# Routing tail on whole fp32 operands, with the gate multiply taken off GpSimd, and a sample GLA state that streams through TensorE

## The chip, the cores and the metric

The kernel runs on one core of one Trainium2 chip. The metric is device time in microseconds (us) of one execution; lower is better. The engines of the core are named as in the profile: PE (TensorE), DVE (VectorE), ACT (ScalarE), POOL (GpSimd) and SP (SyncE, which here only issues DMAs).

## The reference, cut to what matters

One inference step of two layers over 512 prompt tokens and 64 sample tokens (8 sequences of 8). Each layer mixes tokens with three branches (windowed attention, gated linear attention called GLA, causal pooling), merges them, normalises, and applies a PEER layer: each token picks 16 of 16384 one-neuron experts for each of 8 heads.

```
q   = x @ w_query                        # 16 tables of 1024x128: 8 heads x 2 halves
s   = q . sub_keys                       # 128 scores per token, head and half
sv, si = top_k(s, 16);  cand = sv[0][:, None] + sv[1][None, :]
cscore, ci = top_k(cand, 16);  g = softmax(cscore);  eidx = cidx[ci]
h = gelu(u_tab[eidx] . x);  y = sum(g * h * v_tab[eidx])

# GLA, per head and chunk; for a sample sequence S starts from state_gla
o = (q*exp(b)) @ S + causal((q*exp(b)) @ (k*exp(-b)).T) @ v
S = exp(b_last) * S + (k*exp(b_last - b)).T @ v
```

All inputs and outputs are fp32.

## The kernel before

A layer goes through two groups of tokens, one after the other. Group G0 holds 256 prompt tokens and the 64 sample tokens (W = 320 columns), group G1 the other 256 prompt tokens. `_p1` runs the mixing branches and the first norm on one group, `_query` the 16 query tables (`pq`) and the top-16 of each. Matmul operands come in two forms. *Split*: `stream` loads a table `raw` of 128x1024, ACT casts it to `whi` (fp32r), DVE or POOL subtracts to make `wlo`, and `mm_into` runs three passes of 8 matmuls (hi·hi, hi·lo, lo·hi). *Whole*: fp32 operands and one pass of 8 matmuls, each of which the trace shows as two records. `G.nat` says which form a group uses; G1 is whole for attention and GLA, split afterwards. The query tables are split, and POOL makes their `wlo` in G1.

PEER is not gathered for most tokens. For the first 384 tokens a dense loop computes all 128 experts of the first key table (`expert_h`: split `ut` table times `x1A`, 24 matmuls of 384 columns, then Gelu on ACT), multiplies each by a dense gate matrix and accumulates `y`; 24 `y` matmuls of 512 columns follow per expert. The remaining 192 tokens go by gathered rows (`Gather`: `choose`, `fetch`, `weigh`), as background work of DVE and POOL.

The dense gate matrix is written by `_spread`, for 128 tokens at a time: 32 steps of 4 tokens. A step makes two one-hot tiles, `jo` (row index) and `io` (column index times gate), multiplies them on PE (L947) and lets ACT copy the result into four tiles `gst0` to `gst3` (L949). After 8 steps ACT issues four DMAs `gd<-gst` (L955). Tokens 0 to 255 are spread in the background while G1 runs (`pool_mul` off: four `tensor_scalar` on DVE, L943, make `io`). Tokens 256 to 383 are spread in the **tail**, the stretch between G1's query and the dense loop (`pool_mul` on: DVE compares, L939, POOL multiplies by the gate, L940). The program order of the tail is: query of G1, `_slots` (select of tokens 256 to 383, and transposes into `selT`), `h` of the first 12 experts (LA), `_spread`, `choose` for the last 128 tokens at a priority that the code sets, dense loop. The scheduler orders each engine's instructions by program order and priority.

The sample part of GLA works per head on `S0`, the states of 8 sequences (128x8x256), loaded by SP, updated in place by DVE (L550) and stored by ACT (L552). `S0` has one buffer, so a head's load waits until the store of the head before has been read out. Each half `dv` of the output reads `S0` with 8 matmuls of 8 columns:

```
mms += [(po[:, HB + b8 * 8:HB + b8 * 8 + 8], S0[:, b8, dc], qd[:, HB + b8 * 8:HB + b8 * 8 + 8])
        for b8 in range(NB)]
```

`S0[:, b8, dc]` (128x128) is the stationary operand and 8 columns of `qd` move. Both layers run the same code, layer 1 about 2410 us later than layer 0.

Of the kernel before, what the change touches and what calls it, by code (L numbers as in the profile page):

```python
# [10 lines left out]
F32 = mybir.dt.float32  # L11
F32R = mybir.dt.float32r
# [94 lines left out]
class Net:  # L107
# [294 lines left out]
def _phase_gla(n, l, oT):  # L402
    tc, nc, c, G = n.tc, n.nc, n.c, n.G
    W, smp = G.W, G.smp
    with tc.tile_pool(name="gla", side="right", bufs=1) as p, tc.tile_pool(name="gla_u", side="right", bufs=9) as up:
# [10 lines left out]
        for i in range(2):  # L416
            a = p.tile([128, 2, 128], F32, name=f"attT{i}")
            s = p.tile([64, 64], F32, name=f"attS{i}")
            nc.gpsimd.memset(a, 0.0)
            nc.gpsimd.memset(s, 0.0)  # L420
            attT.append((a, s))

# [42 lines left out]
        for h in range(4):  # L465
# [33 lines left out]
            if smp:  # L499
# [3 lines left out]
                                        c["rowm"][0:64, :, None].to_broadcast([64, NB, 128]), op=OP.mult)  # L503
            aT, aS = attT[h % 2]
            pa = n.sm("pa")
# [255 lines left out]
def _p1(n, l, G, xs, xres, dsts, opened=None):  # L761
# [3 lines left out]
    with tc.tile_pool(name="mg", bufs=1) as mp, ExitStack() as xc:  # L765
# [161 lines left out]

def _spread(n, gp, t, sT, new_ps, gt0=None):
    nc, c = n.nc, n.c
    io4 = c["iota"][:, None, :].to_broadcast([128, 4, 128])  # L930
    for g in range(128 // GT):
        st = [gp.tile([128, 32, GT], F32, name=f"gst{i}") for i in range(4)]
        for t4 in range(0, GT, 4):
            tt = g * GT + t4
            jo = gp.tile([128, 4, 128], F32, name="jo", bufs=n.job)
            io = gp.tile([128, 4, 128], F32, name="io", bufs=n.job)
            nc.vector.tensor_tensor(jo, io4, sT[:, 1, tt:tt + 4, None].to_broadcast([128, 4, 128]), op=OP.is_equal)  # L937
            if n.pool_mul:
                nc.vector.tensor_tensor(io, io4, sT[:, 0, tt:tt + 4, None].to_broadcast([128, 4, 128]), op=OP.is_equal)  # L939
                nc.gpsimd.tensor_tensor(io, io, sT[:, 2, tt:tt + 4, None].to_broadcast([128, 4, 128]), op=OP.mult)  # L940
            else:
                for k in range(4):
                    nc.vector.tensor_scalar(io[:, k, :], c["iota"], sT[:, 0, tt + k:tt + k + 1],  # L943
                                            sT[:, 2, tt + k:tt + k + 1], op0=OP.is_equal, op1=OP.mult)
            ps = new_ps().rearrange("p (a b) -> p a b", a=4)
            for k in range(4):
                nc.tensor.matmul(ps[:, k, :], jo[:, k, :], io[:, k, :], start=True, stop=True)  # L947
            for i in range(4):
                nc.scalar.copy(st[i][:, :, t4:t4 + 4], ps[:, :, i * 32:(i + 1) * 32].rearrange("p t i -> p i t"))  # L949
            if t4 + 4 < GT:  # L950
                yield
        if gt0 is not None:
            nc.scalar.copy(gt0[:, t * (128 // GT) + g], st[0][:, 0:4, :])
        for i in range(4):
            nc.scalar.dma_start(n.gd[t * (128 // GT) + g, :, i * 32:(i + 1) * 32, :], st[i])  # L955
        yield
# [72 lines left out]
def tile_hybrid_step(ctx, tc, I, O, L):  # L1029
# [59 lines left out]
    for l in range(L):  # L1089
# [14 lines left out]
        sv, siu = _sel_tiles(sa, 3)  # L1104
        n.job, n.pool_mul = 2, False
        _query(n, l, sa, [n.ks(xa[0]), n.ks(xa[1])], G0.tok, G0.W, sv, siu, n.new_mm)
# [24 lines left out]
        _p1(n, l, G1, [n.ks(x32)], xres, lambda t, c0: [(xb[0], xb[1], c0)],  # L1131
            open_xb)
# [22 lines left out]
        def expert_h(i, eng):
            uh, ul = n.stream(I["ut"][l, i], eng)
            ps = n.hring("ps_h")
            for a, (wt, xi) in enumerate(((uh, 0), (uh, 1), (ul, 0))):
                for k in range(8):
                    nc.tensor.matmul(ps[:, 0:TD], wt[:, k * 128:(k + 1) * 128], x1k[xi][k],  # L1160
                                     start=(a == 0 and k == 0), stop=(a == 2 and k == 7))
# [26 lines left out]
        with tc.tile_pool(name=f"dense{l}", bufs=1) as dp:  # L1188
            gt, late = None, []
            for i in range(NE):  # L1190
# [219 lines left out]
```

## Time and profile before

| | |
|---|---|
| median of 3 runs | 4836.3 us (4829.33 to 4840.92) |
| profiled execution | 4858.47 us, of which its span 4856.7 us |
| mean granted TensorE clock | 0.957 |
| PE busy | 4582.4 us (94%) |
| DVE busy | 3853.8 us (79%) |
| ACT busy | 1869.3 us (38%) |
| POOL busy | 1583.2 us (33%) |

Stages of layer 0 in the trace: G0 up to 600 us, its GLA heads from about 251 to 367; query of G0 to 675; G1 to 1208 with the background spread; tail from 1208 to the first `y` matmul at 1406.80; dense loop to about 2400. In layer 1 the GLA heads stand at about 2660 to 2777, the tail from 3628 to 3830. In the windows view a row gives, for a stretch, the busy time of each engine with its count of instructions, then the granted clock of PE as a share of 2.4 GHz (0.50 is 1.2 GHz), the busy share of the DMA engines and GB/s. In a timeline an x16 row is sixteen like instructions run together, and the bracket behind it is idle time ahead of it with what ended it.

### The profile page before, as it was taken

How to read it: one execution, taken by the hardware profiler on the slowest of the kernel's cores; microseconds unless marked ns; L12 is line 12 of the kernel's file. 1: busy time of each engine (PE TensorE's matmuls, PEld its weight loads, DVE VectorE, ACT ScalarE, POOL GpSimd, SP SyncE). 2: the span in 40 equal slices, each digit the busy share in tenths (PEclk: the TensorE clock that was granted, in tenths of full speed). 3: DMA queues.
4: the chain of work that ended last, by engine and by line, in shares of the span. 5: the costliest groups of instructions: out<-in, count | busy, mean ns of one | idle time of the engine just before them, and what ended most of it. 6: DMA issues, size and time to landing. Idle time of an engine off the chain costs nothing. (4 is left out here: it accounts for less than half of the span.)

```text
span 4856.7 us, 71125 instructions
## 1 busy us (share of the span) xinstructions
PE 4582.4 (94%) x26132; PEld 4105.7 (85%) x26132; DVE 3853.8 (79%) x7303; ACT 1869.3 (38%) x3874; POOL 1583.2 (33%) x996
## 2 busy tenths in 40 slices
PE   7999999998889999999999999999988899999998
PEld 6879886798878999999879799777888789999997
DVE  5445698697989999999864456986979899999998
ACT  3424323354433433333343243234544334333333
POOL 0011001111655555555200110011116555555552
PEclk9979999999999999999999799998999999999999
DMA  4324535576469998988723345255664698988986
GB/s 144 108 94 142 175 108 201 169 251 225 154 227 330 327 330 324 334 322 325 268 87 115 96 140 180 88 209 180 234 231 143 245 327 325 334 321 331 327 325 231
DMA packets 363753, 1095.80 MB, mean 226 GB/s; under 512 B 28622, under 2 KB 168398, under 8 KB 313932
## 3 DMA queue, kind: packets, MB, share of 16 engines
q1 hardware_dynamic: 276336, 610.98, 37.9%
q0 software_dynamic: 55296, 402.68, 22.1%
q10 hardware_dynamic: 31772, 77.60, 4.2%
q8 instruction: 206, 3.38, 0.3%
q14 instruction: 143, 1.17, 0.1%
HBM read 1014.01 MB, written 77.52 MB: 225 GB/s over the span
## 5 line engine op out<-in xcount | busy, mean ns | idle before, releaser
L127 POOL TENSOR_TENSOR wlo<-raw,whi 128x1024 fp32r<-128x1024 f32 x288 | 850.1, 2953 | 796.5 <-ACT whi L130 750.7
L130 ACT CAST whi<-raw 128x1024 fp32r<-128x1024 f32 x638 | 666.4, 1048 | 727.8 <-PE ps_mm L182 363.1
L1160 PE MATMUL ps_h<-x1A,whi 128*128 128x384 f32 x4096 | 776.2, 342 | 35.4 <-ACT h L1163 32.5
L1160 PEld LDWEIGHTS ps_h<-x1A,whi 128*128 128x128 f32 x4096 | 729.1, 192 | 56.1 <-ACT h L1163 36.0
L127 DVE TENSOR_TENSOR wlo<-raw,whi 128x1024 fp32r<-128x1024 f32 x350 | 432.2, 1240 | 293.2 <-PE ps_mm L182 144.5
L990 POOL DMA_INDIRECT uvr<-uv,gidx x384 | 437.9, 1140 | 456.2 <-DVE zB L1008 237.9
L1008 DVE SCALAR_TENSOR_TENSOR zB<-uvr,hc,zB 128x1024 f32<-128x1024 f32 x380 | 566.2, 1490 | 4.7
L1001 DVE SCALAR_TENSOR_TENSOR uvr<-uvr,x1B 128x1024 f32<-128x1024 f32 x384 | 490.5, 1277 | 74.7 <-DMA uvr<-uv,gidx 74.5
L1216 PE MATMUL y<-vh,wh 128*128 128x512 f32 x1536 | 476.5, 392 | 5.4 <-ACT vh L130 5.4
L1216 PE MATMUL y<-vl,wh 128*128 128x512 f32 x1536 | 476.9, 392 | 3.8 <-DVE vl L127 3.8
L1216 PE MATMUL y<-vh,wl 128*128 128x512 f32 x1536 | 474.8, 390 | 0.0
L182 PE MATMUL ps_mm<-xa,whi 128*128 128x320 f32 x2400 | 427.4, 329 | 13.4 <-ACT xa L130 13.4
L1205 DVE TENSOR_TENSOR h<-h,gt 128x384 f32<-128x384 f32 x256 | 402.8, 1579 | 28.9 <-DMA gt<-gd 15.2
L182 PEld LDWEIGHTS ps_mm<-xa,whi 128*128 128x128 f32 x2400 | 382.7, 199 | 38.4 <-issue 19.3
L1160 PE MATMUL ps_h<-x1A,wlo 128*128 128x384 f32 x2048 | 400.4, 338 | 0.0
L1160 PEld LDWEIGHTS ps_h<-x1A,wlo 128*128 128x128 f32 x2048 | 361.2, 189 | 0.1
L1216 PEld LDWEIGHTS y<-vl,wh 128*128 128x128 f32 x1536 | 287.7, 188 | 69.7 <-DVE vl L127 6.6
L1216 PEld LDWEIGHTS y<-vh,wl 128*128 128x128 f32 x1536 | 288.5, 188 | 62.6
L130 ACT CAST wh<-h 128x384 fp32r<-128x384 f32 x256 | 130.6, 512 | 547.1 <-PE y L1216 527.2
L1216 PEld LDWEIGHTS y<-vh,wh 128*128 128x128 f32 x1536 | 286.0, 188 | 49.8 <-ACT vh L130 6.0
L1003 ACT ACTIVATE hc<-hc 128x1 f32<-128x1 f32 x384 | 77.5, 203 | 639.8 <-DVE uvr L1001 625.6
L127 DVE TENSOR_TENSOR vl<-vr,vh 128x1024 fp32r<-128x1024 f32 x256 | 316.0, 1235 | 0.0
(339 smaller groups left out, 7686.2 us busy)
## 6 DMA issues: line engine op xcount, KB each, us to landing
raw<-wall SPq DMA_DIRECT2D x468, 512.0 KB, 3.6
raw<-ut SPq DMA_DIRECT2D x256, 512.0 KB, 5.1
vr<-vt SPq DMA_DIRECT2D x256, 512.0 KB, 6.6
gd<-gst ACTq DMA_DIRECT2D x96, 512.0 KB, 5.0
gt<-gd SPq DMA_DIRECT2D x62, 768.0 KB, 12.2
S<-state_gla SPq DMA_DIRECT2D x8, 1024.0 KB, 7.1
s_gla<-S ACTq DMA_DIRECT2D x8, 1024.0 KB, 4.5
uvr<-uv,gidx POOLq DMA_INDIRECT x384, 8.4
```

What stands on the lines that cost most here:

```text
L127: return eng.tensor_tensor(lo, src, hi.bitcast(F32), op=OP.subtract)
L130: return self.nc.scalar.copy(hi, src), self.sub_lo(lo, src, hi, eng)
L182: self.nc.tensor.matmul(ps[:, 0:W], w[wi][:, k * 128:(k + 1) * 128], xs[xi][k], start=(a == 0 and k == 0), stop=(a == len(pa) - 1 and k == ...
L990: self.n.nc.gpsimd.indirect_dma_start(out=r, out_offset=None, in_=self.n.I["uv"], in_offset=bass.IndirectOffsetOnAxis(ap=self.idx[t][:, s: ...
L1001: nc.vector.scalar_tensor_tensor(r[:, 0:1024], r[:, 0:1024], 1.0, self.x[t], op0=OP.mult, op1=OP.mult, accum_out=hc[:, 0:1])
L1003: nc.scalar.activation(hc[:, 1:2], hc[:, 0:1], AF.Gelu)
L1008: nc.vector.scalar_tensor_tensor(acc, r[:, 1024:2048], hc[:, 1:2], acc, op0=OP.mult, op1=OP.add)
L1160: nc.tensor.matmul(ps[:, 0:TD], wt[:, k * 128:(k + 1) * 128], x1k[xi][k], start=(a == 0 and k == 0), stop=(a == 2 and k == 7))
L1205: nc.vector.tensor_tensor(h3, h3, gt[:, :, i % 4, :], op=OP.mult)
L1216: nc.tensor.matmul(y[t][d], wt[:, ts], vt[:, d * 512:(d + 1) * 512], start=(j == 0 and a == 0), stop=(j == NE - 1 and a == 2))
```

## The change

**Whole query in the tail.** `G.nat` is set back to whole at the end of `_p1`, so G1's query uses the raw tables and `xb` becomes one fp32 pair of tiles; its `wlo`, its ACT cast and the DVE subtraction for `xb` go. The sample-side part of `x1A` is then split by ACT and DVE from `xb` (four DMAs before).

**Whole first 12 experts.** A new pair of tiles `x1W` holds the 384 tokens in fp32 (two POOL additions and two ACT copies). The first 12 experts use it with the raw table and 8 matmuls; the other 116 stay split.

**Spread.** One tile `oh` (two buffers) replaces `jo` and `io` (three buffers in the tail, two in the background); one tile `gst` (one buffer) replaces four; one ACT copy of 128x512 per step replaces four of 128x128. In the tail (`act_mul` = 2) two of the four one-hots are scaled by the gate on ACT, two are made by DVE's `tensor_scalar`; POOL takes no part. The tail's spread is issued at priority 250.

**Sample GLA state.** Per head DVE copies the sample queries into a zeroed, padded tile `qm`; 8 matmuls with 64 padded queries stationary move all of `S0` (256 columns each) into one PSUM tile; ACT copies that to `os`; each half then takes one matmul of `os` with a 64-column identity. `S0` is read by those 8 matmuls alone.

```diff
-            return self.stream(self.I["wall"][l, WPOS[name]], self.nc.gpsimd if self.G.fin and name[0] == "pq" else self.nc.vector,
-                               pool, whole=self.G.nat and name[0] != "pq")
+            return self.stream(self.I["wall"][l, WPOS[name]], self.nc.vector,
+                               pool, whole=self.G.nat)
...
+            if smp:
+                nc.vector.tensor_copy(qm.rearrange("p (b j) -> p b j", b=NB)[:, :, 0:8],
+                                      qd[:, HB:W].rearrange("p (b j) -> p b j", b=NB))
+                pso = n.sm("ps_os", (128, 256))
+                for b8 in range(NB):
+                    nc.tensor.matmul(pso[0:NS], qm[:, b8 * NS:(b8 + 1) * NS], S0[:, b8, :], start=(b8 == 0), stop=(b8 == NB - 1))
+                os = p.tile([NS, 256], F32, name="os", bufs=2)
+                nc.scalar.copy(os, pso[0:NS])
...
-                    mms += [(po[:, HB + b8 * 8:HB + b8 * 8 + 8], S0[:, b8, dc], qd[:, HB + b8 * 8:HB + b8 * 8 + 8])
-                            for b8 in range(NB)]
+                    mms.append((po[:, HB:W], os[:, dc], c["ident"][0:NS, 0:NS]))
...
+    G.nat = G.fin
...
-        st = [gp.tile([128, 32, GT], F32, name=f"gst{i}") for i in range(4)]
+        st = gp.tile([128, 128, GT], F32, name="gst", bufs=n.gst)
...
+            oh = gp.tile([128, 2, 4, 128], F32, name="oh", bufs=n.job)
+            w = n.act_mul
+            for k in range(4):
+                gate = sT[:, 2, tt + k:tt + k + 1]
+                if k < w:
+                    nc.scalar.activation(oh[:, 0, k, :], oh[:, 0, k, :], AF.Copy, scale=gate)
+                else:
+                    nc.vector.tensor_scalar(oh[:, 0, k, :], c["iota"], sT[:, 0, tt + k:tt + k + 1], gate,
+                                            op0=OP.is_equal, op1=OP.mult)
...
-            for i in range(4):
-                nc.scalar.copy(st[i][:, :, t4:t4 + 4], ps[:, :, i * 32:(i + 1) * 32].rearrange("p t i -> p i t"))
+            nc.scalar.copy(st[:, :, t4:t4 + 4], ps.rearrange("p t i -> p i t"))
...
+        x1W = [sp.tile([128, 4, TD], F32, name=f"x1W{q}") for q in range(2)]
+        for q in range(2):
+            nc.gpsimd.tensor_tensor(x1W[q][:, :, 0:HB], x1A[0][q][:, :, 0:HB].bitcast(F32), x1A[1][q][:, :, 0:HB].bitcast(F32),
+                                    op=OP.add)
+            nc.scalar.copy(x1W[q][:, :, HB:TD], xb[q][:, :, 0:TD - HB])
...
-        n.job, n.pool_mul = 3, True
+        n.job, n.gst, n.act_mul = 2, 1, 2
...
-        hs = [expert_h(i, nc.gpsimd) for i in range(LA)]
+        hs = [expert_h(i, x1w) for i in range(LA)]
...
+            with tc.high_priority(SPREAD):
+                for _ in _spread(n, gp, 2, sT2, new_y, gt0):
+                    pass
```

The order in which the engines get their instructions moves in three places. The first is PE in layer 0, first head of the sample GLA; `ps_o` is the output of one half, `S_2192` (in the change `S_2196`) the state S0. Before:

```order
L541 MATMUL ps_o<-qd,S 128x64 x2
L541 MATMUL ps_o<-qd,S_2192 128x8 x8
L548 MATMUL ps_S<-vb,klm 128x256 x2
L541 MATMUL ps_o<-attT_1751,vb 128x128 x2
L541 MATMUL ps_o<-attS_1752,vb 128x64
L541 MATMUL ps_o<-qd,S 128x64 x3
L541 MATMUL ps_o<-qd,S_2192 128x8 x8
```

With the change:

```order
L553 MATMUL ps_o<-qd,S 128x64
L538 MATMUL ps_os<-S_2196,qm_1755 64x256 x8
L553 MATMUL ps_o<-qd,S 128x64
L560 MATMUL ps_S<-vb,klm 128x256
L553 MATMUL ps_o<-ct,os 128x64
L560 MATMUL ps_S<-vb,klm 128x256 x2
L553 MATMUL ps_o<-attT_1751,vb 128x128 x2
```

The state is read once, ahead of the end of the first half, where it was read in both halves.

The second is DVE in the tail of layer 0, where `choose` and the spread meet (`rprod`, `rsum`, `gidx` and the MAX rows are of `choose`). Before, from the end of `choose`:

```order
L848 TENSOR_TENSOR rprod<-rstep,si 128x2048
L852 TENSOR_TENSOR rsum<-rprod 128x1024
L852 TENSOR_TENSOR rprod<-rsum 128x512
L852 TENSOR_TENSOR rsum<-rprod 128x256
L854 TENSOR_TENSOR key_13212<-rsum 128x16x8
L981 TENSOR_TENSOR gidx_11382<-key_13212 128x128
L937 TENSOR_TENSOR jo<-ct,selT_12219 128x512
L939 TENSOR_TENSOR io<-ct,selT_12219 128x512
```

With the change, from the top-16 of `choose`'s sixth head:

```order
L815 MAX cv<-s_12359 128x8
L951 TENSOR_TENSOR oh<-ct,selT_11615 128x512
L953 TENSOR_TENSOR oh<-ct,selT_11615 128x256
L960 TENSOR_SCALAR oh<-ct,selT_11615 128x128 x2
L951 TENSOR_TENSOR oh<-ct,selT_11615 128x512
L953 TENSOR_TENSOR oh<-ct,selT_11615 128x256
L960 TENSOR_SCALAR oh<-ct,selT_11615 128x128 x2
L816 MAX_INDEX ciu<-cv,s_12359 128x8
L813 MAX_INDEX ciu<-cv,cand 128x8
```

Before, 29 of the 32 steps stood behind the whole of `choose`; now 11 stand among its top-16 rows and others among its sums.

The third is ACT in the same tail, at the end of the first eight steps (`gst` the collecting tile, `gd` its DMA, `ps_yr` the PSUM result). Before:

```order
L949 COPY gst_12727<-ps_yr 128x32x4
L949 COPY gst_12728<-ps_yr 128x32x4
L949 COPY gst_12729<-ps_yr 128x32x4
L949 COPY gst_12730<-ps_yr 128x32x4
L953 COPY gt_12220<-gst_12727 128x128
L955 DMA gd<-gst_12727 128x1024
L955 DMA gd<-gst_12728 128x1024
L955 DMA gd<-gst_12729 128x1024
L955 DMA gd<-gst_12730 128x1024
L949 COPY gst_12848<-ps_yr 128x32x4
```

With the change:

```order
L958 ACTIVATE oh<-oh,selT_11615 128x128 x2
L965 COPY gst<-ps_yr 128x128x4
L969 COPY gt_11616<-gst 128x128
L971 DMA gd<-gst 128x1024 x4
L958 ACTIVATE oh<-oh,selT_11615 128x128 x4
L1182 ACTIVATE h<-ps_h 128x384
L919 ACT_TABLE_LOAD
L919 ACTIVATE g_12417<-g_12417 128x128
L965 COPY gst<-ps_yr 128x128x4 x3
```

Four tiles released one by one have become a single tile that all four DMAs read, and two scales stand ahead of each copy; four stand between the DMAs and the next copy.

## Rows read from the trace of the kernel before

**Rows 1.** Part 1 of the page: busy time, share of the span, instructions.

```profile
PE 4582.4 (94%) x26132; PEld 4105.7 (85%) x26132; DVE 3853.8 (79%) x7303; ACT 1869.3 (38%) x3874; POOL 1583.2 (33%) x996
```

**Rows 2.** Windows view: G0's GLA, layers 0 and 1, and G1's GLA (900:960).

```profile
300.00:310.00 10.00, 10.00 (x27) 6.86 (x28) 2.72 (x7) 1.09 (x5) 0.00 (x0) 0.50 0.00 0
...
240.00:380.00 140.00, 135.91 (x637) 111.19 (x636) 63.46 (x107) 33.30 (x64) 15.35 (x17) 0.74 0.31 100
2640.00:2780.00 140.00, 135.98 (x644) 111.10 (x643) 60.61 (x101) 28.40 (x56) 14.82 (x17) 0.74 0.30 97
900.00:960.00 60.00, 52.64 (x303) 43.59 (x301) 42.45 (x93) 29.38 (x83) 11.26 (x12) 0.91 0.46 152
```

**Rows 3.** Timeline of PE in the GLA stage: start, us, operation, count.

```profile
262.59 4.86 PE L541 MATMUL ps_o<-qd,S 128*128 128x64 f32 x22
...
324.22 1.84 PE L541 MATMUL ps_o<-qd,S 128*128 128x8 f32 x16
...
367.36 4.36 PE L182 MATMUL ps_mm<-xa,whi 128*128 128x320 f32 x16
```

**Rows 4.** Part 6 of the page: DMA issues, KB each, us from issue to landing.

```profile
gd<-gst ACTq DMA_DIRECT2D x96, 512.0 KB, 5.0
...
S<-state_gla SPq DMA_DIRECT2D x8, 1024.0 KB, 7.1
s_gla<-S ACTq DMA_DIRECT2D x8, 1024.0 KB, 4.5
```

**Rows 5.** Tile view of S in layer 0's G0: duration ns min/median/max.

```profile
L550 DVE SCALAR_TENSOR_TENSOR S<-S,dec,ps_S x32: 472/479/482, 264.5 to 367.9; 128x256 f32<-128x256 f32 x32
```

**Rows 6.** Timeline of PE: a whole table in G1, then the tail of layer 0.

```profile
820.89 12.76 PE L182 MATMUL ps_mm<-oa,raw 128*128 128x256 f32 x58 [0.15 <-DMA raw<-wall]
...
1217.34 2.17 PE L182 MATMUL ps_yr<-xb,whi 128*128 128x256 f32 x16
...
1220.30 0.61 PE L812 MATMUL ps_sc<-key,qT 128*128 128x128 f32 x4
1220.66 1.56 PE L182 MATMUL ps_yr<-xb,whi 128*128 128x256 f32 x11
...
1263.46 1.39 PE L812 MATMUL ps_sc<-key,qT 128*128 128x128 f32 x8
...
1270.57 2.94 PE L1160 MATMUL ps_h<-x1A,whi 128*128 128x384 f32 x16
...
1274.73 2.94 PE L1160 MATMUL ps_h<-x1A,whi 128*128 128x384 f32 x16
...
1340.50 1.12 PE L947 MATMUL ps_yr<-io,jo 128*128 128x128 f32 x8
1341.38 0.42 PE L1160 MATMUL ps_h<-x1A,whi 128*128 128x384 f32 x1
...
1406.80 1.66 PE L1216 MATMUL y<-vh,wh 128*128 128x512 f32 x6 [2.71 <-ACT vh L130]
```

**Rows 7.** Windows view of layer 0's tail: select, choose, spread.

```profile
1270.00:1300.00 30.00, 23.04 (x122) 22.40 (x121) 29.89 (x134) 11.68 (x16) 12.52 (x5) 0.89 0.25 88
1300.00:1333.00 33.00, 30.55 (x177) 30.23 (x175) 32.38 (x66) 14.86 (x25) 23.77 (x11) 0.95 0.38 124
1333.00:1392.00 59.00, 42.24 (x272) 35.87 (x272) 58.73 (x59) 22.45 (x116) 38.12 (x30) 0.94 0.31 118
```

**Rows 8.** Groups of DVE in 1333:1392: count, busy us, mean ns, idle before.

```profile
L939 DVE TENSOR_TENSOR io<-ct,selT 128x512 f32<-128x512 f32 x29 | 43.3, 1494 | 0.0
L937 DVE TENSOR_TENSOR jo<-ct,selT 128x512 f32<-128x512 f32 x29 | 19.7, 679 | 0.0
```

**Rows 9.** Groups of DVE: one sum in 1270:1333, then in 640:860.

```profile
L852 DVE TENSOR_TENSOR rprod<-rsum 128x512 bf16<-128x512 bf16 x6 | 9.1, 1515 | 0.1
...
L852 DVE TENSOR_TENSOR rprod<-rsum 128x512 bf16<-128x512 bf16 x6 | 3.0, 508 | 0.0
```

**Rows 10.** Timeline of DVE in the background spread.

```profile
1090.16 1.10 DVE L943 TENSOR_SCALAR io<-ct,selT 128x128 f32<-128x128 f32 x4
```

**Rows 11.** Groups of ACT in 1333:1392, with idle time by what ended it.

```profile
L949 ACT COPY gst<-ps_yr 128x128 f32<-128x128 f32 x113 | 22.1, 285 | 35.7 <-PE ps_yr L947 23.2 <-DMA gd<-gst 12.3
```

More of the change, by code (lines that the diff above doesn't have):

```diff
@@ L46 @@
 LAGB = -50
+SPREAD = 250
 C_QA, C_KA, C_VA, C_QB, C_KB, C_VB, C_LR, C_GB, C_UC, C_GT = (
@@ L420, in _phase_gla @@
             nc.gpsimd.memset(s, 0.0)
-            attT.append((a, s))
+            qm = p.tile([128, NB * (NS + 8)], F32, name=f"qm{i}") if smp else None
+            if smp:
+                nc.gpsimd.memset(qm, 0.0)
+            attT.append((a, s, qm))
         ps = n.pmm.tile([128, 512], F32, tag="mm", name="ps_lr", bufs=3)
@@ L503, in _phase_gla @@
                                         c["rowm"][0:64, :, None].to_broadcast([64, NB, 128]), op=OP.mult)
-            aT, aS = attT[h % 2]
+            aT, aS, qm = attT[h % 2]
             pa = n.sm("pa")
@@ L929, in _spread @@
     nc, c = n.nc, n.c
-    io4 = c["iota"][:, None, :].to_broadcast([128, 4, 128])
+    iota = lambda w: c["iota"][:, None, None, :].to_broadcast([128, w, 4, 128])
     for g in range(128 // GT):
-        st = [gp.tile([128, 32, GT], F32, name=f"gst{i}") for i in range(4)]
+        st = gp.tile([128, 128, GT], F32, name="gst", bufs=n.gst)
         for t4 in range(0, GT, 4):
             tt = g * GT + t4
[L935 to L944, printed above, removed]
+            oh = gp.tile([128, 2, 4, 128], F32, name="oh", bufs=n.job)
+            w = n.act_mul
+            nc.vector.tensor_tensor(oh[:, 1], iota(1)[:, 0], sT[:, 1, tt:tt + 4, None].to_broadcast([128, 4, 128]), op=OP.is_equal)
+            if w:
+                nc.vector.tensor_tensor(oh[:, 0, 0:w], iota(1)[:, 0, 0:w], sT[:, 0, tt:tt + w, None].to_broadcast([128, w, 128]),
+                                        op=OP.is_equal)
+            for k in range(4):
[5 more added lines that the diff above has]
+                                            op0=OP.is_equal, op1=OP.mult)
@@ L945, in _spread @@
             ps = new_ps().rearrange("p (a b) -> p a b", a=4)
             for k in range(4):
-                nc.tensor.matmul(ps[:, k, :], jo[:, k, :], io[:, k, :], start=True, stop=True)
-            for i in range(4):
-                nc.scalar.copy(st[i][:, :, t4:t4 + 4], ps[:, :, i * 32:(i + 1) * 32].rearrange("p t i -> p i t"))
+                nc.tensor.matmul(ps[:, k, :], oh[:, 1, k, :], oh[:, 0, k, :], start=True, stop=True)
+            nc.scalar.copy(st[:, :, t4:t4 + 4], ps.rearrange("p t i -> p i t"))
@@ L952, in _spread @@
         if gt0 is not None:
-            nc.scalar.copy(gt0[:, t * (128 // GT) + g], st[0][:, 0:4, :])
+            nc.scalar.copy(gt0[:, t * (128 // GT) + g], st[:, 0:4, :])
         for i in range(4):
-            nc.scalar.dma_start(n.gd[t * (128 // GT) + g, :, i * 32:(i + 1) * 32, :], st[i])
+            nc.scalar.dma_start(n.gd[t * (128 // GT) + g, :, i * 32:(i + 1) * 32, :], st[:, i * 32:(i + 1) * 32, :])
         yield
@@ L1104, in tile_hybrid_step @@
         sv, siu = _sel_tiles(sa, 3)
-        n.job, n.pool_mul = 2, False
+        n.job, n.gst, n.act_mul = 2, 1, 0
         _query(n, l, sa, [n.ks(xa[0]), n.ks(xa[1])], G0.tok, G0.W, sv, siu, n.new_mm)
@@ L1125, in open_xb @@
             xbp = xbc.enter_context(tc.tile_pool(name=f"xb{l}", side="right", bufs=1))
-            xb.extend([xbp.tile([128, 4, G1.W], F32R, name=f"xb{i}{q}") for q in range(2)] for i in range(2))
+            xb.extend(xbp.tile([128, 4, G1.W], F32, name=f"xb{q}") for q in range(2))
         n.early = EARLY
@@ L1143, in tile_hybrid_step, with expert_h @@
                 nc.sync.dma_start(x1A[i][q][:, :, 0:HB].bitcast(F32), x1h[i, q])
-                nc.sync.dma_start(x1A[i][q][:, :, HB:TD].bitcast(F32), xb[i][q][:, :, 0:128].bitcast(F32))
+        for q in range(2):
+            n.split(x1A[0][q][:, :, HB:TD], x1A[1][q][:, :, HB:TD], xb[q][:, :, 0:TD - HB])
         x1k = [n.ks(x1A[0]), n.ks(x1A[1])]
         sc, sp = scope(f"sel{l}")
+        x1W = [sp.tile([128, 4, TD], F32, name=f"x1W{q}") for q in range(2)]
+        for q in range(2):
+            nc.gpsimd.tensor_tensor(x1W[q][:, :, 0:HB], x1A[0][q][:, :, 0:HB].bitcast(F32), x1A[1][q][:, :, 0:HB].bitcast(F32),
+                                    op=OP.add)
+            nc.scalar.copy(x1W[q][:, :, HB:TD], xb[q][:, :, 0:TD - HB])
+        x1w = [n.ks(x1W)]
         sv, siu = _sel_tiles(sp, 2)
-        n.job, n.pool_mul = 3, True
+        n.job, n.gst, n.act_mul = 2, 1, 2
         yc, n.py = scope(f"ps_y{l}", space=PSUM)
         new_y = lambda: n.py.tile([128, 512], F32, tag="y", name="ps_yr", bufs=6)
-        _query(n, l, sp, [n.ks(xb[0]), n.ks(xb[1])], G1.tok, G1.W, sv, siu, new_y)
+        _query(n, l, sp, [n.ks(xb)], G1.tok, G1.W, sv, siu, new_y)
         xbc.close()
         rc.close()
[L1155 to L1161, printed above, removed]
+        def expert_h(i, xs):
+            w = n.stream(I["ut"][l, i], nc.gpsimd, whole=len(xs) == 1)
+            ps = n.mm_into(n.hring("ps_h"), w, xs, TD)
             h = ep.tile([128, TD], F32, name="h", bufs=LA + 2)
-            nc.scalar.activation(h, ps[:, 0:TD], AF.Gelu)
+            nc.scalar.activation(h, ps, AF.Gelu)
             return h
@@ L1196, in tile_hybrid_step @@
                 if i + LA < NE:
-                    hs.append(expert_h(i + LA, nc.gpsimd))
+                    hs.append(expert_h(i + LA, x1k))
                 vr = dp.tile([128, 1024], F32, name="vr", bufs=3)
```

5 lines of the change are left out of this document (2 added, 3 removed).

## The prediction


> **What bounds the kernel now.** I read the page's busy times first: PE works 94% of the span and DVE 79% [rows 1], so whatever shortens the run must remove PE time, or idle or slow-clocked PE time. The windows view says where such time lies. The change touches two places per layer. In G0's GLA stage PE is busy 135.91 of 140 us at a mean clock of 0.74, in layer 1 the same [rows 2]: it is slow-clocked, and stretches like 300 to 310 run at 0.50, the 1.2 GHz level, while PE is busy all the time. In layer 0's tail the first `y` matmul comes at 1406.80 [rows 6], while DVE is busy 29.89 of 30, 32.38 of 33 and 58.73 of 59 us [rows 7]. So DVE's queue ends last there, and PE waits for it. In the dense loop, which I did not find touched otherwise, PE is the bound.
>
> How much PE time the tail loses follows from the timeline. G1's query ends at 1263.46 + 1.39 = 1264.85 [rows 6]. Up to 1406.80 PE does 13 experts' `h` at 1274.73 − 1270.57 = 4.16 us, 54.1 us together, and 32 spread steps at 1341.38 − 1340.50 = 0.88 us, 28.2 us. Back to back that ends at 1347.2, so **59.6 us are lost** to waits, broken bursts and a lowered clock (0.89, 0.95, 0.94 [rows 7]).
>
> **The change part by part.**
>
> *Whole operands cost PE time.* A whole table's record of 256 columns takes 12.76 / 58 = 0.220 us [rows 6]. A query table is 8 matmuls, 16 records, 3.52 us; the split one takes 1220.30 − 1217.34 = 2.96 us. That is +0.56, and 16 tables give +9. The first 12 experts move 384 columns; no row has a whole record of that width, so I scale by columns: 0.330 us, 16 records 5.28 us against 4.16, +1.12, and 12 of them +13.4. Sum **+23 us per layer**, all on PE; for the scaling by columns I keep 18 to 28.
>
> The Trainium skill speaks against this. In "FP8 and Floating Point Precision", section "TensorE Precision Notes", it counts true FP32 as four passes through the array; against the three split passes that would be 2.96 × 4/3 = 3.95 us per table and 4.16 × 4/3 = 5.55 per expert, an estimate of +32 us per layer. The row on whole tables disagrees for 256 columns (3.52 us); for 384 columns nothing here shows it.
>
> *What the tail gets back.* POOL's part is removed. Beside POOL's multiply DVE's L939 takes 1494 ns where L937, the same compare, takes 679 [rows 8]: 29 × 0.815 = 23.6 us of DVE. The same stretching hits `choose` and select while POOL subtracts tables: 512-column products take 1515 ns in the tail and 508 in the background [rows 9], 6 us in this group alone. A new spread step on DVE is a full compare (0.68 [rows 8]), half a compare (0.34) and two `tensor_scalar` at 1.10 / 4 = 0.275 [rows 10]: 1.57 us against 59 / 29 = 2.03. Over 32 steps this saves 15 us. DVE's queue from 1270 to 1392 [rows 7] shrinks from 121.0 to 100 us, and with a query that ends 9 us later its end moves from 1392 to about 1380.
>
> PE's new queue up to the first `y`: query end 1274; 12 whole experts 63.4; 32 steps 28.2; the order puts some 4.3 split experts ahead of the first `y`, 18. That ends near 1384, with 16.3 experts done, not 13. Against before it is 23 us earlier and 3.3 × 4.16 = 13.7 us further: 36.6 us, which is 59.6 less 23. PE becomes the bound by a few us, and DVE follows close behind.
>
> Not all of it will come. One `gst` tile must be free before the next group's first copy, so ACT now waits for all four DMAs (landing 5.0 us [rows 4]) after issuing them, and scales and Gelus queue behind that copy. ACT's waits on these DMAs were 12.3 us in the tail [rows 11]; with four tiles released in turn they were mostly hidden by DVE. I let these 12.3 us stand as PE stalls: **−24 us per layer**. The bounds are −36.6 (nothing stalls) and the serial step of the rivals. The copies themselves get cheaper: 113 copies took 22.1 us [rows 11] and become some 29 wider ones, of ACT time that is off the path.
>
> *Sample GLA state.* 128x8 records take 1.84 / 16 = 0.115 us at full clock [rows 3]; a head has 32, 3.7 us. New: 16 records of 256 columns, 3.5, and four narrow ones, about 0.4. The work is equal; what may change is the clock. At 262.59 a run of 22 records, 16 of them narrow, takes 4.86 us [rows 3], about twice its full-clock time, and the clock is low behind it; the three later heads look alike. G1's GLA stage, the same code without the 8-column matmuls, runs at 0.91 [rows 2]. If G0 reaches this, 140 us become 140 × 0.74 / 0.91 = 114: −26. Two new hand-overs per head (DVE to PE, PE to ACT to PE) take some back: **−24 per layer**. The bounds are −36 (clock 1.00) and +2 (clock unchanged). Below 114 the state's own loop is next: reading 3.5, eight updates at 0.48 [rows 5] with as many matmuls between them, some 6.5 together, store 4.5 and load 7.1 [rows 4], 21.6 us per head. Three turns after the first read at about 259, and 12 us for the last head, end at 336 where the stage ended at 367.36 [rows 3]: this caps the gain at 31.
>
> *The rest.* The background spread keeps its DVE work. Its ACT copies get fewer, but the single `gst` adds waits; ACT is 38% busy over the span, so I put this at 0, between −4 and +6. The `x1W` additions and copies hide under the query; uncovered they would cost four operations of some 3 us. SP loses four loads, which hide in a stage where it is not the bound.
>
> **Sum.** (24 + 24) × 2 = 96 us off 4858.47 gives 4762 for a profiled execution. The median stands at 4836.3 / 4858.47 = 0.9954 of it, so the forecast is **4741 us**.
>
> **The rivals.** Times are on the median's basis.
>
> *The GLA clock stays low.* For it: PE is busy while its clock is 0.50, so I know what runs when it falls, not why. Stalls on the new state loop could also bring it down. Against: G1's 0.91. GLA then gives +2 instead of −24: 4792 us.
>
> *The tail pays for its own query only.* The hand-overs between DVE, ACT and PE keep a step near its old 2 us, or the `gst` boundary costs double. What is recovered about matches the 23 us of extra PE work, −5 per layer: 4779 us. For it speaks that two `oh` buffers replace three of each one-hot; against, that DVE, the old bound, gets some 21 us lighter.
>
> *Everything arrives.* −36.6 and −31 per layer: 4702 us.
>
> *Whole operands cost a third more than split ones.* An expert then takes 4.16 × 4/3 = 5.55 us and a table 2.96 × 4/3 = 3.95, together 10 us more per layer than forecast: 4760 us. The row on whole tables, 3.52 us, is against it. By the page named above it is what should happen.
>
> *Slower: the spread step becomes serial.* Place: the tail's loop DVE, ACT scale, PE, ACT copy. ACT works in order, and the copy of one step stands ahead of the scales of a later one. If each step waits out the whole round, it takes about 1.6 + 0.5 + 0.9 + 0.6 = 3.6 us where it took 2.03. Per layer this is 32 × 1.57 = +50, +9 for the longer query, −6 for the unstretched sums and −16 for experts that run in the gaps: +37, less the 24 of GLA: +13, so 4862 us. It decides from 3.2 us per step on. Against: the order has scales two steps ahead of the copies, which lets two steps overlap.
>
> **How the numbers follow.** Forecast 0.42; a third more 0.03; GLA clock stays 0.15; tail pays only for itself 0.20; everything arrives 0.10; serial step 0.06; both gains absent, within 0.2% (9.7 us, about what a measurement tells from no change) 0.04. Range 4700 to 4800: it reaches from "everything arrives" to the two weaker cases, and leaves out the serial step, no change and the worse ends of the weaker ones. Faster 0.90, same 0.04, slower 0.06.
>
> **What would show it.** In the profile after: the windows of 240 to 380 should show a clock near 0.9 and `gb` starting about 24 us before 367; low clock with the new matmuls refutes that step. Whole experts should show records near 0.33 us, query tables 3.5 us. DVE's full compare should be near 0.6 to 0.68 in every tail step, a step 1.6 to 1.9 us; PE's first `y` within 1375 to 1400 less the GLA gain, with more experts done. ACT's waits on `gd<-gst` near 12 us in the tail; much more, or PE waiting on `oh`, is the second rival or the serial step. The forecast is wrong if DVE is not what PE waits for, since then lightening it frees nothing.

## The result and the profile after

The changed kernel takes 4735.1 us (median of 4 runs, 4729.2 to 4743.1), the kernel before 4838.6. The ratio is 0.9782 with a 95% interval of 0.9767 to 0.9797: faster by 103.5 us in the medians. The profiled execution has a span of 4735.2 us against 4856.7. The forecast was 4741.

Busy times, to be read beside [rows 1]:

```profile
PE 4530.7 (96%) x25588; PEld 4001.3 (85%) x25588; DVE 3793.4 (80%) x7435; ACT 1820.2 (38%) x3386; POOL 1370.1 (29%) x884
```

PE is busy 52 us less, though whole operands gave it more work: its slow-clocked time went. That shows in the windows of the GLA stage, of layer 0 ([rows 2] before); the second row is its one remaining dip:

```profile
240.00:380.00 140.00, 135.33 (x780) 111.96 (x779) 82.55 (x137) 50.90 (x95) 15.72 (x18) 0.98 0.40 131
...
320.00:330.00 10.00, 7.26 (x21) 4.13 (x22) 7.40 (x11) 0.00 (x0) 0.00 (x0) 0.66 0.34 107
```

The clock is 0.98 where it was 0.74, and more work fits into the same 140 us (780 records, 637 before). The stage begins with the transposes of its first head, at 251.17 before and at 248.88 now, and ends where the first table matmul behind the last state update starts, at 367.36 before [rows 3] and at 338.66 now. It is 26.4 us shorter (116.2 and 89.8 us). Timeline of PE, the first row before the change and the others with it:

```profile
251.17 0.44 PE L495 MATMUL pt<-ct,ekl 128*128 128x128 f32 x2 [1.28 <-POOL ekl L491]
...
248.88 0.44 PE L499 MATMUL pt<-ct,ekl 128*128 128x128 f32 x2 [1.29 <-POOL ekl L495]
...
325.63 5.29 PE L538 MATMUL ps_os<-S,qm 128*64 128x256 f32 x16 [0.95 <-DVE oT L594]
...
338.66 2.77 PE L183 MATMUL ps_mm<-xa,whi 128*128 128x320 f32 x16
```

The tail of layer 0 in PE's timeline, beside [rows 6]:

```profile
1179.84 3.62 PE L183 MATMUL ps_yr<-xb,raw 128*128 128x256 f32 x16
1183.29 0.61 PE L825 MATMUL ps_sc<-key,qT 128*128 128x128 f32 x4
1183.74 3.62 PE L183 MATMUL ps_yr<-xb,raw 128*128 128x256 f32 x16
...
1301.13 6.62 PE L183 MATMUL ps_h<-x1W,raw 128*128 128x384 f32 x20
1307.59 1.95 PE L964 MATMUL ps_yr<-oh 128*128 128x128 f32 x16
...
1368.47 2.37 PE L1236 MATMUL y<-vh,wh 128*128 128x512 f32 x6
```

A query table now takes 1183.74 − 1179.84 = 3.90 us with its scores, 3.32 before. A whole record of 384 columns takes (1307.59 − 1301.13) / 20 = 0.323 us. The query starts at 1169.38, 39.3 us earlier than before, and the first `y` comes 38.3 us earlier: from query to first `y` nothing was gained, but more experts are done by then (counted below).

What PE waits for there, from the waits view of 1235 to 1369 (total us, times, longest):

```profile
PE ps_yr L964 <- ACT oh L958: 6.4, 6, 2.2
PE ps_h L183 <- ACT h L1182: 4.6, 1, 4.6
PE ps_yr L935 <- DVE key L867: 2.2, 1, 2.2
```

And the windows, to be read beside [rows 7]:

```profile
1265.00:1300.00 35.00, 34.21 (x187) 25.43 (x186) 34.68 (x116) 23.47 (x57) 0.00 (x0) 1.00 0.32 108
1300.00:1330.00 30.00, 28.92 (x131) 20.13 (x130) 17.22 (x34) 12.75 (x27) 8.86 (x4) 1.00 0.59 212
1330.00:1369.00 39.00, 29.77 (x164) 28.58 (x165) 24.73 (x46) 20.15 (x45) 9.77 (x4) 0.84 0.56 208
```

From 1265 to 1300 PE and DVE are both full. From 1300 on DVE is busy 17 of 30 us: it no longer bounds the tail. PE does, until the whole experts end near 1325; from 1330 on it is busy 29.77 of 39 us at a clock of 0.84, with waits for the last steps' scales.

### The profile page after: what moved, and what is told of

Its sections match the earlier page's. It is cut to its first block, busy times and chain, and to the rows that moved or that the text cites. A ratio compares the mean times of both kernels' runs of the same rounds, so it can differ in the third digit from the quotient of the medians.

```text
span 4735.2 us, 69451 instructions
## 1 busy us (share of the span) xinstructions
PE 4530.7 (96%) x25588; PEld 4001.3 (85%) x25588; DVE 3793.4 (80%) x7435; ACT 1820.2 (38%) x3386; POOL 1370.1 (29%) x884
## 5 line engine op out<-in xcount | busy, mean ns | idle before, releaser
L128 POOL TENSOR_TENSOR wlo<-raw,whi 128x1024 fp32r<-128x1024 f32 x232 | 704.1, 3035 | 928.4 <-ACT whi L131 894.1
L131 ACT CAST whi<-raw 128x1024 fp32r<-128x1024 f32 x582 | 607.9, 1048 | 601.0 <-PE ps_mm L183 379.0
L183 PE MATMUL ps_h<-x1A,whi 128*128 128x384 f32 x3712 | 696.4, 340 | 13.3 <-ACT h L1182 13.2
L183 PEld LDWEIGHTS ps_h<-x1A,whi 128*128 128x128 f32 x3712 | 655.9, 190 | 33.6 <-ACT h L1182 17.1
L1024 DVE SCALAR_TENSOR_TENSOR zB<-uvr,hc,zB 128x1024 f32<-128x1024 f32 x380 | 587.2, 1545 | 4.7
L183 PE MATMUL ps_mm<-xa,whi 128*128 128x320 f32 x2400 | 413.3, 321 | 14.7 <-ACT xa L131 14.7
L183 PEld LDWEIGHTS ps_mm<-xa,whi 128*128 128x128 f32 x2400 | 370.7, 194 | 33.8 <-ACT xa L131 15.3
L183 PE MATMUL ps_h<-x1A,wlo 128*128 128x384 f32 x1856 | 362.7, 338 | 0.0
L183 PEld LDWEIGHTS ps_h<-x1A,wlo 128*128 128x128 f32 x1856 | 327.1, 189 | 0.0
```

What stands on the lines that cost most here:

```text
L128: return eng.tensor_tensor(lo, src, hi.bitcast(F32), op=OP.subtract)
L131: return self.nc.scalar.copy(hi, src), self.sub_lo(lo, src, hi, eng)
L183: self.nc.tensor.matmul(ps[:, 0:W], w[wi][:, k * 128:(k + 1) * 128], xs[xi][k], start=(a == 0 and k == 0), stop=(a == len(pa) - 1 and k == ...
L1024: nc.vector.scalar_tensor_tensor(acc, r[:, 1024:2048], hc[:, 1:2], acc, op0=OP.mult, op1=OP.add)
```

## The experiments

Two measures follow. The **ratio** is that of the runs to those of the kernel before. The **stretch** is read from each profiled execution's timeline of PE: from the first matmul of G1's query to the last `y` matmul of the layer, tail and dense loop together. Nothing in the GLA stage touches it, and kernels that differ only there agree in it within 4 us.

| kernel | median us | ratio, 95% interval | stretch, layers 0 and 1, us |
|---|---|---|---|
| before | 4838.6 | 1 | 1210.4, 1210.5 |
| the change | 4735.1 | 0.9782 [0.9767, 0.9797] | 1196.6, 1197.2 |
| e1 new GLA alone | 4776.9 | 0.9866 [0.9846, 0.9887] | 1210.0, 1206.7 |
| e2 all but the GLA | 4794.6 | 0.9902 [0.9885, 0.9920] | 1194.5, 1197.6 |
| e3 experts split | 4755.3 | 0.9816 [0.9798, 0.9834] | 1207.3, 1203.6 |
| e4 experts and query split | 4744.3 | 0.9795 [0.9777, 0.9813] | 1197.3, 1197.9 |
| e5 narrow matmuls again | 4848.3 | 1.0009 [0.9998, 1.0020] | 1197.6, 1198.7 |
| e6 POOL multiplies | 4776.2 | 0.9872 [0.9856, 0.9888] | 1209.2, 1214.8 |
| e7 no priority | 4804.0 | 0.9924 [0.9910, 0.9938] | 1228.4, 1228.4 |
| e8 query split, whole experts | 4731.5 | 0.9773 [0.9751, 0.9796] | 1186.7, 1188.5 |
| e9 e1 with priority on the old spread | 4758.4 | 0.9818 [0.9797, 0.9838] | 1198.9, 1202.7 |
| e10 gates on DVE | 4723.9 | 0.9754 [0.9738, 0.9771] | 1190.7, 1190.9 |
| e11 e8 with three oh buffers | 4728.5 | 0.9758 [0.9743, 0.9772] | 1189.0, 1186.1 |
| e12 e8 and e10 together | 4717.7 | 0.9736 [0.9723, 0.9749] | 1181.3, 1186.9 |

### e1 and e2: the two halves

e1 is the kernel before with these lines of the change (and those that make `qm` and `os`); e2 is the changed kernel without them.

```diff
-                    mms += [(po[:, HB + b8 * 8:HB + b8 * 8 + 8], S0[:, b8, dc], qd[:, HB + b8 * 8:HB + b8 * 8 + 8])
-                            for b8 in range(NB)]
+                    mms.append((po[:, HB:W], os[:, dc], c["ident"][0:NS, 0:NS]))
```

> The kernel before with the new sample GLA alone. My theory (the narrow 8-column matmuls go with the low clock, and the two gains add up): the GLA stage ends 24 to 29 us earlier in each layer at a clock near 1.0, and nothing behind it takes that back; 4838 - 55 = about 4783 us. Rival (the state only streams at a high clock because something else in the change is there, or the gain is absorbed later): 4825 to 4838 us.

> The changed kernel with the sample GLA of before. My theory: the low clock of 0.74 is back in 240 to 380 us, 4735 + 55 = about 4790 us. Rival (the parts overlap, so that taking one away costs less than it gave alone): 4750 to 4770 us.

The GLA alone gives 1.34%, 65 us or 32 per layer; the rest alone 0.98%, 47 us. Together 112, against 105 by the ratio of the whole change: they add up within the intervals, as the theory had it, and each rival falls. e2's window shows the low clock back; it also shows that the clock differs between executions of the same code (0.74 before):

```profile
240.00:380.00 140.00, 136.68 (x683) 114.10 (x683) 68.59 (x116) 38.12 (x74) 15.59 (x17) 0.79 0.33 108
```

### e5: is it the narrow matmuls or the way the state is held?

```diff
+                if smp:
+                    mms += [(po[:, W + b8 * 8:W + b8 * 8 + 8], Ss[1 + b8 % 4][:, dc], qd[:, HB + b8 * 8:HB + b8 * 8 + 8])
+                            for b8 in range(NB)]
```

> The changed kernel, with 8 more 8-column matmuls per half and head put into the output tile's unused columns; they read the prompt's states, not S0, so the sample state's loop is as in the change, and their results are not used. They are 16 records of 0.115 us at full clock, 1.84 us per half, 15 us per layer. Theory (the 8-column runs go with the low clock): the clock of 240 to 380 us falls to about 0.75 again, the stage is 35 to 40 us longer per layer, about 4735 + 75 = 4810 us. Rival (the low clock came from the way S0 was held, the narrow matmuls are just work): the clock stays near 0.98 and the time grows by their own 15 us per layer at most, 4750 to 4765 us.

Windows view, both layers:

```profile
240.00:380.00 140.00, 135.94 (x599) 106.66 (x598) 54.39 (x93) 27.06 (x55) 13.14 (x14) 0.73 0.25 83
2640.00:2780.00 140.00, 138.10 (x678) 112.41 (x677) 51.83 (x91) 29.96 (x57) 13.43 (x14) 0.77 0.27 91
```

With the state's loop as in the change, the clock falls to 0.73 as soon as runs of 8-column matmuls are back. The run is 113 us above the change, 57 per layer. The GLA stage alone, measured as above, takes 141 us in layer 0 and 139 in layer 1 against 90 and 91: some 50 us more, for 15 us of added work at full clock, so about 35 us per layer of stage time go with the low clock. I had expected 35 to 40 in all; I had not let the added work itself run at the low clock. The rival, that the narrow matmuls are just work and the clock stays near 0.98, is out. What in a narrow run lowers it was not tried.

### e6 and e9: POOL's multiply

e6 in the tail of the changed kernel (w = 4, no ACT scale):

```diff
-                if k < w:
-                    nc.scalar.activation(oh[:, 0, k, :], oh[:, 0, k, :], AF.Copy, scale=gate)
+                if w:
+                    if k == 0:
+                        nc.gpsimd.tensor_tensor(oh[:, 0], oh[:, 0], sT[:, 2, tt:tt + 4, None].to_broadcast([128, 4, 128]), op=OP.mult)
```

> The changed kernel with the tail's gate multiply on POOL again (DVE makes two full compares, POOL multiplies 128x512; order, tiles and whole operands as changed). Theory (DVE's second compare stretches beside POOL, and DVE is close behind PE): a step costs DVE 2.0 to 2.1 us and not 1.57, 32 steps some 15 us per layer, most of which shows: 4755 to 4765 us. Rival (PE is the bound of the new tail, so DVE has room): 4735 to 4742 us.

Groups of DVE from 1236 to 1380, PE's first wait of that stretch, and a window of it:

```profile
L951 DVE TENSOR_TENSOR oh<-ct,selT 128x512 f32<-128x512 f32 x32 | 32.7, 1022 | 15.5 <-PE ps_yr L965 15.5
L953 DVE TENSOR_TENSOR oh<-ct,selT 128x512 f32<-128x512 f32 x32 | 30.7, 958 | 0.0
```

```profile
PE ps_yr L965 <- POOL oh L959: 21.6, 24, 4.7
```

```profile
1300.00:1330.00 30.00, 22.66 (x123) 14.88 (x122) 29.42 (x38) 7.72 (x15) 16.70 (x12) 1.00 0.35 128
```

The two compares take 1.98 us a step, as expected, and PE waits 21.6 us for POOL. It costs 0.9%, 41 us in the medians (20 to 30 expected), and 13 to 18 us per layer of stretch. The rival, that DVE has room, is out: DVE is busy 29.42 of 30 us and PE 22.66. How much of the cost is DVE's longer step and how much POOL's own place in the round to PE, the run does not separate.

e9 leaves the old spread (POOL, four `gst`, three buffers) and the split operands, and gives the spread the priority, on top of e1:

```diff
-            for _ in _spread(n, gp, 2, sT2, new_y, gt0):
-                pass
+            with tc.high_priority(SPREAD):
+                for _ in _spread(n, gp, 2, sT2, new_y, gt0):
+                    pass
```

> The kernel before with the new sample GLA and the priority of 250 on the old spread (POOL multiplies, four gst tiles, three buffers, operands split). To be read between e1 (4777 us, no priority) and e4 (4744 us, new spread with priority). Theory (the order is the larger part, as e7 against e6 has it, and the lighter step the smaller): 4755 to 4765 us. Rival 1 (the order alone is the gain): 4744 us. Rival 2 (without the lighter step DVE stays the bound and the order frees nothing): 4775 us or more.

Between e1 (0.9866) and e4 (0.9795) lies 0.9818: as the theory had it, the priority alone gives about two thirds of what priority and new spread give together. Its gain over e1 is clear of the intervals; that e4 is better than e9 is not, and rests on the stretch, 2 and 5 us. PE still waits 19.0 us for POOL (1220 to 1480):

```profile
PE ps_yr L959 <- POOL io L952: 19.0, 17, 2.5
```

### e7: the order

The changed kernel without the priority (e9's diff the other way).

> The changed kernel without the priority of the tail's spread, so that choose comes ahead of most of its steps again. Theory (the gain is the lighter DVE queue, its inner order matters little): 4735 to 4745 us. Rival (the gain is the order: the spread early among choose's top-16 rows keeps PE fed): 10 us or more per layer, 4755 us and up.

It costs 69 us, 31 us per layer of stretch, and leaves the stretch 18 us **longer** than before the change. The rival is right, and by far. Windows of layer 0, waits of PE from 1240 to 1407, and DVE's compare from 1300 to 1400:

```profile
1241.00:1309.00 68.00, 64.30 (x196) 37.51 (x196) 46.16 (x236) 15.75 (x25) 3.87 (x3) 0.97 0.29 102
...
1330.00:1370.00 40.00, 28.74 (x166) 26.34 (x165) 22.46 (x48) 18.97 (x44) 7.44 (x3) 0.80 0.36 129
1370.00:1406.00 36.00, 18.67 (x88) 16.77 (x88) 19.52 (x48) 16.63 (x41) 0.00 (x0) 0.69 0.39 148
```

```profile
PE ps_yr L964 <- ACT oh L958: 23.2, 14, 6.0
PE ps_h L183 <- ACT h L1182: 9.6, 1, 9.6
```

```profile
L951 DVE TENSOR_TENSOR oh<-ct,selT 128x512 f32<-128x512 f32 x30 | 21.2, 707 | 49.3 <-PE ps_yr L964 48.9 <-ACT oh L958 0.4
```

Up to 1309 PE runs 196 records: that is all 12 whole experts (192) and the transposes of select, and no spread step. DVE had made two steps by 1272, and from 1300 on it waits 48.9 us for PE to read the tiles. When PE reaches the spread at 1309 no whole expert is left to put between the steps; the split ones of the order end at 1350, and from there the round DVE, ACT, PE is paid bare: PE is busy 18.67 of 36 us at a clock of 0.69. DVE is not the bound there. So, as this trace reads, the priority pays less by where it puts the steps on DVE, which I had read, than by where it puts them on PE.

### e3, e4 and e8: what the whole operands are worth

e3 builds the first 12 experts split again:

```diff
-        hs = [expert_h(i, x1w) for i in range(LA)]
+        hs = [expert_h(i, x1k) for i in range(LA)]
```

e4 splits the query too, as before the change. e8 keeps whole experts, splits the query as e4 does, and makes `x1W` later, in memory that G1 has left:

```diff
+        wc, wpool = scope(f"x1w{l}", side="right")
+        x1W = [wpool.tile([128, 4, TD], F32, name=f"x1W{q}") for q in range(2)]
+        for q in range(2):
+            nc.gpsimd.tensor_tensor(x1W[q], x1A[0][q].bitcast(F32), x1A[1][q].bitcast(F32), op=OP.add)
```

> The changed kernel with the first 12 experts split again (POOL subtracts their low parts, 24 matmuls each). My theory: PE has 13 us less work per layer, but POOL's 12 subtractions stretch DVE's select, choose and spread by about 12 us per layer and DVE is the bound again; about 4735 + 10 = 4745 us. Rival (whole experts are a pure cost to PE, DVE has room): 4735 - 26 = 4709 us.

> The changed kernel with query and first 12 experts both split as before; the new spread, its priority and the new GLA stay. Against e3 only the query differs. My theory: the query ends 9 to 10 us earlier per layer and POOL's subtractions within it fall on DVE's top-k rows, which are not stretched; 20 us less than e3, about 4725 us. Rival (whole query also takes work from DVE that matters: the xb subtraction and the stretched rows): the same time as e3 or more.

> The changed kernel with the query split as before and the 12 whole experts kept; x1W is made by two POOL additions over all 384 columns, in memory that the layer's prompt tiles leave. Theory (e4 against e3: the whole query only costs PE time): 9 to 10 us of PE per layer come back, most of it shows, 4735 - 12 to - 19, about 4720 us. Rival (with whole experts the tail behind the query is bound by DVE and takes the time back): 4735 us.

Split experts cost 11 and 6 us of stretch though PE has less to do: PE waits 12.3 us for ACT's scales and 9.3 for select's `key`, 6.4 and 2.2 with whole ones. These are e3's waits from 1236 to 1380:

```profile
PE ps_yr L964 <- ACT oh L958: 12.3, 9, 4.9
PE ps_yr L935 <- DVE key L867: 9.3, 2, 7.1
```

A split query gives 6 to 10 us of stretch back, with split experts (e4) and with whole ones (e8, 10 and 9). By the stretch, then, the 12 whole experts pay and the whole query does not: in e4 they cancel, and its ratio is not told apart from the change's. e8's ratio is not either, though its stretch is shorter in both layers. Each stretch is one execution, and the medians came out above what I expected of all three: e3 by 10 us, e4 by 19, e8 by 11.

### e10, e11 and e12: the round trip

e10 lets DVE make all gated one-hots in the tail:

```diff
-        n.job, n.gst, n.act_mul = 2, 1, 2
+        n.job, n.gst, n.act_mul = 2, 1, 0
```

e11 is e8 with three `oh` buffers (first number 3, third 2) and LA = 11. e12 is e8 with e10's line.

> The changed kernel with all four gated one-hots of a step made by DVE's tensor_scalar (act_mul 0 in the tail), so that ACT stands in no step between DVE and PE. Theory (behind choose DVE waits for PE and PE for ACT's scales, the length of the round counts): PE's 6.4 us of waits on ACT's oh per layer go, 4725 to 4732 us. Rival (DVE is the bound of the first 16 steps, where a step grows from 1.57 to about 1.7 us): 4738 to 4745 us.

> e8 (query split, 12 whole experts) with three oh buffers in the tail instead of two, and 11 early experts instead of 12 to make room. Theory (DVE's 12 us of waits for an oh that PE still reads, and PE's for the next, come from two buffers): 3 to 6 us less per layer than e8's 4731.5, 4720 to 4726 us. Rival (the steps wait for in-order ACT and for gst, not for oh): 4731 us or more.

> e8 and e10 together: query split, 12 whole experts with late x1W, all gates of the tail's spread by DVE. Theory (both gains are PE time that nothing takes back): e10's 4724 less the 4 us that e8 gave, down to 10 us less where the shorter query shows in full: 4714 to 4720 us. Rival (with POOL busy in the query and DVE full in the spread, DVE's queue ends last again): 4724 us or more.

e10 takes 6 us off the stretch of each layer. DVE's step grows from 1.46 to 1.63 us where no row of `choose` stands in it, but PE's wait of 6.4 us for ACT becomes one of 3.5 us for DVE, in 1220 to 1480:

```profile
PE ps_yr L964 <- DVE oh L960: 3.5, 2, 2.2
```

The median is a microsecond under the range expected, but the run does not show that the hand-over to ACT was what cost: most of the 6.4 us stood behind long compares of DVE (shown below), and e10 has fewer of those. Its ratio 0.9754 [0.9738, 0.9771] just touches the change's interval. e11 misses its expectation: 4728.5 us, not told apart from e8, stretch +2 and −2 us. DVE's wait for PE to read an `oh` is 12.0 us still (12.2 in the change), so a third buffer did not take it away; what the one early expert less cost, the run does not separate. e12 is **4717.7 us, ratio 0.9736 [0.9723, 0.9749]**, clear of the change's interval and the lowest of all, 17 us under the change; it is not told apart from e10.

## Why the prediction was right

The time is 6 us from the forecast. Both mechanisms were right, but that the number is so near is in part luck: the GLA gave more than forecast and the tail less, and in the tail's term three errors offset each other in part.

**GLA, −24 per layer: mechanism right, size near.** The stage got 26.4 us shorter in layer 0 and 26.6 in layer 1, and 25 in each layer of e1. I had taken G1's clock, 0.91, as what could be reached; it became 0.98, and the gain stayed under the cap of 31 that I had worked out from the state's loop. What is left of the loop shows at 320 to 330, where PE is busy 7.26 of 10 us and the clock falls for once. e1's ratio gives 32 us per layer, so some 7 of them lie outside the stage as profiled; no run shows where.

**Whole operands, +23 per layer: right.** A table costs 3.90 − 3.32 = 0.58 more (0.56 forecast), the query 65.7 us from first matmul to last scores against 55.9. A whole record of 384 columns takes 0.323 us (0.330 by scaling). An expert is then 16 × 0.323 = 5.17 us against 4.16, which is 1.24 times. Together that is 22 us per layer. The Trainium skill's four passes ("FP8 and Floating Point Precision", "TensorE Precision Notes") would have made it 4/3, an estimate of 5.55 us; the measurement decides, and that rival is out.

**The tail, −24 per layer: too large.** The stretch got 14 and 13 us shorter. The first step that failed is the count that gave 59.6 us of lost PE time: I put 13 experts ahead of the old first `y`. The groups of PE in the tail before (1264 to 1407) show 15:

```profile
L1160 PE MATMUL ps_h<-x1A,whi 128*128 128x384 f32 x240 | 53.7, 369 | 7.7 <-ACT h L1163 6.3 <-DVE s L801 1.4
...
L1160 PE MATMUL ps_h<-x1A,wlo 128*128 128x384 f32 x119 | 24.4, 347 | 0.0
```

240 + 119 records (the last one stands just behind the first `y`) are 15 experts of 24, 62.4 us and not 54.1. That makes 51.3 us lost.

The second is the 12.3 us that I left as stalls. In the new tail 133.1 us pass from the query's end at 1235.38 to the first `y` at 1368.47. 12 whole experts take 62.0 of them, 32 steps 28.2, and 4.33 split experts (104 records) 18.0, so 24.9 us are lost, twice what I left. PE is idle for 14.7 of these (13 in the three rows of waits above); the rest is lower clock and broken bursts. ACT's waits on `gd`, where I had looked for the stalls, were 12 us as forecast, but only 6.8 of them stand ahead of copies (1260 to 1370):

```profile
ACT gst L965 <- DMA gd<-gst: 6.8, 3, 3.2
ACT wh L131 <- DMA gd<-gst: 2.9, 1, 2.9
ACT oh L958 <- DMA gd<-gst: 2.7, 1, 2.7
```

So 51.3 − 24.9 = 26.4 us were recovered, 22 of them paid for whole operands, and some 4.5 us were gained up to the first `y`: it comes 1 us later after the query's start, with 16.33 experts done and not 15, 5.5 us of work. The other 9 us came where the sum has no term, in the dense loop behind the first `y`. There PE waited for Gelus; the first row is from before (1406.8 to 2419), the second with the change (1368.47 to 2366):

```profile
PE ps_h L1160 <- ACT h L1163: 10.0, 3, 6.3
...
PE ps_h L183 <- ACT h L1182: 2.4, 2, 2.0
```

PE is idle 9 us in that loop in e1, which keeps the old tail, 2 and 5 us in e9, which has only the priority besides, and 3 and 5 us in e7, which lacks the priority alone. Either the priority or the rest of the tail's change thus takes most of this idle time away; how was not tried.

**DVE as what PE waits for: half right.** A step costs DVE about what I said; this one is 1.57 us from compare to compare, with a row of `choose` in it (timeline of DVE):

```profile
1268.31 0.68 DVE L951 TENSOR_TENSOR oh<-ct,selT 128x512 f32<-128x512 f32 x1
1268.91 0.42 DVE L953 TENSOR_TENSOR oh<-ct,selT 128x256 f32<-128x256 f32 x1
1269.24 0.60 DVE L960 TENSOR_SCALAR oh<-ct,selT 128x128 f32<-128x128 f32 x2
1269.76 0.20 DVE L815 MAX8 cv<-s 128x8 f32<-128x50 f32 x1
1269.88 0.67 DVE L951 TENSOR_TENSOR oh<-ct,selT 128x512 f32<-128x512 f32 x1
```

e6 confirms that POOL's multiply is worth 13 to 18 us per layer. But I credited the lighter queue with the whole gain and gave the priority no price. e7 prices it: 31 us per layer, without which the rest of the tail's change loses 18. My PE queue silently took the new order for granted, with experts left to fill the spread. Behind 1300 DVE has idle time, yet single compares of it still hold PE. The one at 1327.34 takes 2.60 us, the same compare 0.42 in the rows above, while POOL subtracts the tables of split experts, and PE's next wait ends behind it (DVE, POOL, PE):

```profile
1327.34 2.60 DVE L953 TENSOR_TENSOR oh<-ct,selT 128x256 f32<-128x256 f32 x1
...
1324.49 5.16 POOL L128 TENSOR_TENSOR wlo<-raw,whi 128x1024 fp32r<-128x1024 f32 x2 [3.13 <-ACT whi L131]
...
1330.48 0.49 PE L964 MATMUL ps_yr<-oh 128*128 128x128 f32 x2 [1.56 <-ACT oh L958]
```

Two more such compares, of 2.6 us each, stand ahead of PE's waits of 2.20 and 1.90 us. So 5.7 of the 6.4 us put down to ACT's scales come behind DVE rows that are long beside POOL's subtraction, a stretching for which my sum had no term there.

**The rivals.** The low clock did not stay (e1). That the tail pays for its own query only, −5 us per layer, was nearer to the 13 or 14 of the stretch than my −24, though the `gst` boundary did not cost double. Not everything arrived: the stretch got nowhere near −36.6. The serial step did not come: steps overlap, 1.57 us in the one shown. Its neighbour did in e7, where the round trip is paid bare and the tail ends slower than before, by another cause than the one I named.

**The rest, 0.** G1 with its background spread takes 515 to 528 us in the layers of the eleven kernels with the new one and 518 to 543 in those of the three profiled with the old one (before, e1, e9). Some 5 us per layer may lie there; single profiled executions don't settle it.

So 26 in the GLA stage, 13 in tail and dense loop, and some 12 of the medians' 52 us per layer that no run places in a stage stand where 24, 24 and 0 were forecast.

## What to carry to other kernels

When work of a bounded stage is made lighter, price its order apart from its weight: here the same instructions were 31 us per layer better or worse by whether fill work stood ahead of the dependent steps on PE or between them. Count the work done at a milestone from grouped records and not by following a few rows, and look behind the milestone too: two thirds of what the tail's changes gained here came after the first `y`. And look for busy stretches at a low granted clock as one looks for idle ones: they were the larger half of this gain (e1 against e2).

## What the hardware showed

The granted clock fell to the 1.2 GHz level while PE was busy all the time (10.00 of 10.00 us at 0.50 [rows 2]), ahead of it runs of 8-column matmuls. Before the change a first run, 16 of its 20 records narrow, goes at full clock, and the next, at 262.59 [rows 3], takes twice as long:

```profile
257.96 2.40 PE L541 MATMUL ps_o<-qd,S 128*128 128x64 f32 x20
```

The clock was 0.98 over 240 to 380 when the same products were made from 256-column matmuls, and 0.73 again when 8-column runs on other operands were added (e5). I had not expected a PE that hardly waits (135.94 of 140 us busy in e5) to lose some 35 us per layer to its clock.
